# A gated delta rule inside a projection stage: side work pinned between numbered matmuls, decays loaded through GpSimd's queue, and a shorter triangular substitution

## The chip, the cores and the metric

The kernel runs on one core of one Trainium2 chip. The metric is the device time of one execution in microseconds (us); lower is better. In the profile TensorE is PE (its weight loads are PEld), VectorE is DVE, ScalarE is ACT, GpSimd is POOL and SyncE, which issues nearly all DMAs, is SP.

## The reference, cut to what matters

Two decoder layers over 1024 tokens of width 1024. Each layer normalises the residual, projects it once into many pieces, runs a sparse attention branch and a gated delta rule branch, mixes both by gates and projects back. The change concerns the delta rule branch:

```python
qkv_b = jax.nn.silu(causal_depthwise_conv(qkv_b, conv_w[layer]))
q_b = l2_normalize(q_b...); k_b = l2_normalize(k_b...)
beta = jax.nn.sigmoid(beta_l)
g = -jnp.exp(a_log[layer]) * jax.nn.softplus(a_l + dt_bias[layer])
# per head, in chunks:  S_t = a_t (I - b_t k_t k_t^T) S_{t-1} + b_t k_t v_t^T,  o_t = S_t^T q_t,  a_t = exp(g_t)
decay = jnp.exp(jnp.where(incl, gc[..., :, None] - gc[..., None, :], -jnp.inf))
lower = jnp.where(strict, (kb @ k^T) * decay, 0.0);  tmat = I + lower
u, w = triangular_solve(tmat, v * beta), triangular_solve(tmat, kb * exp(gc))
v_new = u - w @ state
o = (q * exp(gc)) @ state + ((q @ k^T) * decay) @ v_new
state = state * g_tot + k_dec^T @ v_new
y_b = rms_norm(o_b, gdn_norm_gain) * silu(z_b)
```

There are 8 heads of width 128. The kernel works in 8 chunks of 128 tokens.

## The kernel before, in words

Each layer has three stages. `token_phase` makes the token-major projections and the top-k selection. `feature_phase` makes, feature-major, the conv inputs of q, k, v and the gates, and runs the delta rule beside them. `attention` does the sparse attention and half of the output projection.

`feature_phase` is the stage that the change touches. It consists of 2208 projection matmuls of 128x128 by 128x512 (`proj_feat`, L361; 24 of them fill one PSUM bank), fed by weights that SP loads (`w_raw`, L303), ACT rounds (`w_hi`, L139) and DVE subtracts (`w_lo`, L140). A head takes 144 of them for its three convolutions (k, q, v in this order) and 96 for its two gates; the gates of a head are projected one head later, in `gdn_finish`. Everything else of a head is side work:

- `decay_rows` loads the head's decay rows, spread to all partitions (512 KB, `H<-rows`, issued by SP at L665), masks them on POOL (L666) and takes the exponent on ACT in eight pieces (L669). The tile `H` has three buffers, so the load for head h+1 waits until head h-2 has finished with its own.
- `gdn_front` convolves (ACT copies L687 and L688, DVE L694 three times, ACT L696, DVE L697), transposes k, q and v (L708), takes their norms (ACT L723), scales `kdec` and `vb` (DVE L713) and forms the products k k^T and q k^T (L758, L760, L761).
- `inverse_blocks` inverts the 32x32 diagonal blocks: it sends them through DRAM into a layout with one row set per partition, does 31 substitution steps of two DVE instructions each on all eight row groups (L847, L849), and sends the result back through DRAM (L851, and 16 small loads at L855).
- `inverse_pairs` joins the blocks by small matmuls (L871 to L893).
- `gdn_chunks` is the recurrence: per chunk `pk` (L780), `r` on DVE, `pu` (L784), `u` on DVE (L786), `pn` (L789), the new state on DVE (L794), and the output from two products in two halves of a bank, which DVE scales and adds (L797 to L803).
- `gdn_finish` scales the output (L821), transposes it (L825), multiplies by the gate and stores it to `yb`.

The order in each engine's queue is not written by hand. A planner orders instructions by priority (the order of the program, shifted by `high_priority(offset)`) and by its own estimate of when their inputs are ready; each engine then works through its queue in order and waits at an instruction whose inputs are late. PE's queue before therefore has the side work wherever the planner expected it to be ready.

Of the kernel before, what the change touches and what calls it, by code (L numbers as in the profile page):

```python
# [25 lines left out]
F32 = mybir.dt.float32  # L26
# [4 lines left out]
AF = mybir.ActivationFunctionType  # L31
# [5 lines left out]
P = 128  # L37
# [31 lines left out]
AHEAD, BEHIND = 1000, -10  # L69
# [17 lines left out]
class Trunk:  # L87
    def __init__(self, ctx, tc, args):
# [10 lines left out]
        self.beside = None  # L99
        ctx.enter_context(self.banks(acc=(1, 2), tr=(1, 2)))  # L100
# [49 lines left out]
    def constants(self, first):  # L150
# [25 lines left out]
        for q in range(4):  # L176
            nc.gpsimd.affine_select(self.xinit[32 * q:32 * q + 32], self.xinit[32 * q:32 * q + 32],
                                    pattern=[[1, 8], [-1, 32]], compare_op=OP.not_equal, fill=1.0, base=8 * q,
                                    channel_multiplier=0)
# [113 lines left out]


# [59 lines left out]
    def proj_feat(self, ws, half, act, evac, tag="acc"):  # L354
# [3 lines left out]
        for k in range(KT):  # L358
            cs = slice((k % 4) * P, (k % 4 + 1) * P)
            for i, (a, b) in enumerate(((0, 0), (0, 1), (1, 0))):  # L360
                self.nc.tensor.matmul(acc, ws[k // 4][a][:, cs], act[b][:, k, hs], start=k == 0 and i == 0,  # L361
                                      stop=k == KT - 1 and i == 2)
        evac(hs, acc)
        self.tick()
# [48 lines left out]
    def decays(self, l, p, raw):  # L413
# [41 lines left out]
        row = p.tile([64, P], F32, name="row")  # L455
        nc.vector.tensor_copy(row, pr[:64, :P])
        self.rows = self.dram.tile([T, 8, P], F32, name="rows")
        nc.sync.dma_start(out=self.rows.rearrange("t h c -> (t h) c"), in_=row)
# [180 lines left out]
    def feature_phase(self, l, ht):  # L639
        nc, tc = self.nc, self.tc  # L640
        self.yb = self.dram.tile([HEADS, P, S], F32, name="yb")
        with tc.tile_pool(name="feat", bufs=1) as p, self.banks(ch=(1, 2), oc=(1, 1), more=(1, 1)):
            XF = p.tile([P, T, 64], F32, name="xf")
            nc.gpsimd.memset(XF, 0.0)
            heads = {}
            E = self.decay_rows(p, 0)
            for h in range(HEADS + 1):
                if h < HEADS:
                    H, E = E, self.decay_rows(p, h + 1) if h + 1 < HEADS else None
                    heads[h] = self.gdn_front(l, p, ht, h, H)  # L650
# [4 lines left out]
                if h:  # L655
                    self.gdn_finish(l, p, ht, heads.pop(h - 1))
                if h < HEADS:
                    self.gdn_chunks(p, heads[h], XF)

    def decay_rows(self, p, h):  # L660
# [4 lines left out]
        nc.sync.dma_start(out=E, in_=ap(self.rows, h * P, [[0, P], [8 * P, T], [1, P]]))  # L665
# [6 lines left out]
    def gdn_front(self, l, p, ht, h, H):  # L672
        nc = self.nc
        w = self.w_in[l]
        feat = self.feat[l]
        kf = p.tile([P, S], F32, name="kf", bufs=3)
        qf = p.tile([P, S], F32, name="qf", bufs=3)
        vv = p.tile([P, S], F32, name="vv", bufs=1)
        for base, dst in ((1024, kf), (0, qf), (2048, vv)):
            ct = (base + h * P) // P  # L680
            cw = lambda j: feat[:, 24 * j + ct:24 * j + ct + 1]
            xp = p.tile([P, S + 4], F32, name="xp", bufs=2)
            nc.gpsimd.memset(xp[:, 0:4], 0.0)

            def evac(hs, acc):
                o = hs.start
                nc.scalar.copy(xp[:, 4 + o:516 + o], acc)  # L687
                nc.scalar.activation(dst[:, hs], acc, AF.Copy, scale=cw(3))  # L688

            ws = self.feat_weights(w, C_QKVB + base + h * P)  # L690
            for half in range(2):
                self.proj_feat(ws, half, ht, evac)
            for j in range(3):
                nc.vector.scalar_tensor_tensor(dst, xp[:, 1 + j:1 + j + S], cw(j), dst, op0=OP.mult, op1=OP.add)  # L694
            th = xp[:, 4:4 + S]
            nc.scalar.activation(th, dst, AF.Tanh, scale=0.5)  # L696
            nc.vector.scalar_tensor_tensor(dst, th, 1.0, dst, op0=OP.add, op1=OP.mult)  # L697

        sm = self.small
        beta, egc, egs = (a[:, :, h] for a in (self.beta, self.egc, self.egs))  # L700
        kdec = p.tile([P, T, P], F32, name="kdec", bufs=2)
        vb = p.tile([P, T, P], F32, name="vb", bufs=2)

        def turn(src, half):
            pt = self.tr()
            for i in range(4):
                c = 4 * half + i
                nc.tensor.transpose(pt[:, i * P:(i + 1) * P], src[:, c * P:(c + 1) * P], self.ident)  # L708
            return pt

        def scaled(dst, pt, col, half):
            cs = slice(4 * half, 4 * half + 4)
            nc.vector.tensor_mul(dst[:, cs], pt.rearrange("p (c d) -> p c d", c=4),  # L713
                                 col[:, cs, None].to_broadcast([P, 4, P]))

        ssq = sm.tile([P, 16], F32, name="g_ssq")
        for i, src in enumerate((kf, qf)):
            for half in range(2):
                pt = turn(src, half)
                for c in range(4):  # L720
                    junk = p.tile([P, P], F32, name="g_junk", bufs=1)
                    col = 8 * i + 4 * half + c
                    nc.scalar.activation(junk, pt[:, c * P:(c + 1) * P], AF.Square, accum_out=ssq[:, col:col + 1])  # L723
                if i == 0:
                    scaled(kdec, pt, egs, half)
        v16 = sm.tile([P, 16], F32, name="g_v16")
# [419 lines left out]
```

## Time and profile before

| | |
|---|---|
| median of 3 runs | 2730.17 us (2725.91 to 2731.36) |
| the profiled execution's own time | 2725.06 us, span 2723.3 us |
| PE busy in the span | 2570.7 us, 94% |
| DVE busy | 1972.8 us, 72% |
| ACT busy | 1316.8 us, 48% |
| POOL busy | 111.9 us, 4% |
| `feature_phase`, first and second layer | about 370 to 1101 us and 1718 to 2455 us |

Busy time is the time in which an engine executed instructions; a matmul's end is modelled, and consecutive matmuls overlap, so a busy PE is read from the distance of the starts. "PEclk" in the views is the granted TensorE clock as a share of 2.4 GHz. A wait is idle time of an engine ahead of an instruction, put down to what ended it.

### The profile page before, as it was taken

How to read it: one execution, taken by the hardware profiler on the slowest of the kernel's cores; microseconds unless marked ns; L12 is line 12 of the kernel's file. 1: busy time of each engine (PE TensorE's matmuls, PEld its weight loads, DVE VectorE, ACT ScalarE, POOL GpSimd, SP SyncE). 2: the span in 40 equal slices, each digit the busy share in tenths (PEclk: the TensorE clock that was granted, in tenths of full speed). 3: DMA queues.
4: the chain of work that ended last, by engine and by line, in shares of the span. 5: the costliest groups of instructions: out<-in, count | busy, mean ns of one | idle time of the engine just before them, and what ended most of it. 6: DMA issues, size and time to landing. Idle time of an engine off the chain costs nothing.

```text
span 2723.3 us, 42939 instructions
## 1 busy us (share of the span) xinstructions
PE 2570.7 (94%) x14854; PEld 2140.5 (79%) x14854; DVE 1972.8 (72%) x5450; ACT 1316.8 (48%) x3169; POOL 111.9 (4%) x398
## 2 busy tenths in 40 slices
PE   7999989999999999999999999898999999999998
PEld 7677778777777888898786777686887778888986
DVE  6677967767787775697366888677676777757965
ACT  5579643343333332697245894433333343227962
POOL 0122000000000000000001210000000000000000
PEclk9999999999999999999999999998899999999999
DMA  3113332222222221531420232321212221226324
GB/s 121 48 66 90 85 87 56 49 51 57 61 51 53 50 73 51 174 105 35 157 65 30 78 101 71 77 63 47 53 42 65 51 57 46 69 63 180 92 68 143
DMA packets 283262, 202.95 MB, mean 75 GB/s; under 512 B 55906, under 2 KB 241188, under 8 KB 283044
## 3 DMA queue, kind: packets, MB, share of 16 engines
q1 hardware_dynamic: 283044, 200.20, 26.2%
q8 instruction: 117, 1.92, 0.3%
q14 instruction: 101, 0.83, 0.1%
HBM read 153.80 MB, written 46.33 MB: 73 GB/s over the span
## 4 chain that ended last, share of the span: by engine, by line
PE 68%; DVE 13%; ACT 7%; DMA 6%; issue 5%; POOL 1%; SPq 0%; DVEq 0%; POOLq 0%; ACTq 0%
PE acc L361 20%; PE acc L338 11%; PE more L361 9%; PE acc L1038 4%; PE wide L1006 4%; PE tr L758 2%; PE tr L1029 2%; ACT t_junk L562 2%; PE out L338 2%; ACT g_junk L723 2%; DMA w_raw<-in_w_in_dram 2%; DVE t_junk L544 2%; DVE w_lo L140 2%; DMA H<-rows 2%; PE tr L708 1%
## 5 line engine op out<-in xcount | busy, mean ns | idle before, releaser
L361 PE MATMUL acc<-hi_t,w_hi 128*128 128x512 f32 x1240 | 502.2, 405 | 8.3 <-DVE gate L629 7.3
L361 PE MATMUL acc<-hi_t,w_lo 128*128 128x512 f32 x1240 | 501.9, 405 | 0.0
L361 PE MATMUL acc<-lo_t,w_hi 128*128 128x512 f32 x1240 | 499.6, 403 | 0.0
L139 ACT CAST w_hi<-w_raw 128x512 fp32r<-128x512 f32 (+1 forms) x336 | 201.1, 602 | 371.0 <-PE acc L361 196.8
L140 DVE TENSOR_TENSOR w_lo<-w_raw,w_hi 128x512 fp32r<-128x512 f32 (+1 forms) x336 | 223.3, 668 | 149.2 <-ACT w_hi L139 136.0
L338 PE MATMUL acc<-w_hi,hi_t 128*128 128x512 f32 (+1 forms) x768 | 285.7, 373 | 12.6 <-ACT w_hi L139 7.3
L338 PE MATMUL acc<-w_lo,hi_t 128*128 128x512 f32 (+1 forms) x768 | 284.5, 371 | 2.1 <-DVE w_lo L140 1.9
L338 PE MATMUL acc<-w_hi,lo_t 128*128 128x512 f32 (+1 forms) x768 | 283.6, 369 | 0.0
L361 PEld LDWEIGHTS acc<-hi_t,w_hi 128*128 128x128 f32 x1240 | 236.7, 191 | 49.8 <-DVE gate L629 8.6
L361 PEld LDWEIGHTS acc<-hi_t,w_lo 128*128 128x128 f32 x1240 | 236.2, 190 | 41.1
L361 PEld LDWEIGHTS acc<-lo_t,w_hi 128*128 128x128 f32 x1240 | 236.3, 191 | 40.9
L562 ACT ACTIVATE t_junk<-scores,t_bits 128x640 f16<-128x640 f32 x248 | 198.8, 802 | 30.8 <-DVE t_bits L554 26.0
L361 PE MATMUL more<-hi_t,w_hi 128*128 128x512 f32 x488 | 198.8, 407 | 4.5 <-ACT kf L688 4.5
L361 PE MATMUL more<-hi_t,w_lo 128*128 128x512 f32 x488 | 199.2, 408 | 0.0
L361 PE MATMUL more<-lo_t,w_hi 128*128 128x512 f32 x488 | 198.3, 406 | 0.0
L338 PEld LDWEIGHTS acc<-w_hi,hi_t 128*128 128x128 f32 x768 | 146.2, 191 | 40.6 <-ACT w_hi L139 10.5
L338 PEld LDWEIGHTS acc<-w_lo,hi_t 128*128 128x128 f32 x768 | 146.7, 191 | 27.4 <-DVE w_lo L140 5.1
L338 PEld LDWEIGHTS acc<-w_hi,lo_t 128*128 128x128 f32 x768 | 146.6, 191 | 22.0 <-issue 1.0
L544 DVE TENSOR_SCALAR_CACHE_REDUCE t_junk<-scores,t_bits 128x1024 f16<-128x1024 f32 (+4 forms) x136 | 153.4, 1128 | 4.3
L849 DVE TENSOR_TENSOR xc<-xc,xtmp 128x248 f32<-128x248 f32 (+30 forms) x496 | 141.8, 286 | 3.1
L847 DVE TENSOR_TENSOR xtmp<-wide,xc 128x248 f32<-128x248 f32 (+30 forms) x496 | 141.6, 285 | 2.7
L806 ACT ACTIVATE o_junk<-vb 128x128 f32<-128x128 f32 x128 | 39.6, 310 | 162.3 <-DVE vb L803 126.3
(344 smaller groups left out, 5478.4 us busy)
## 6 DMA issues: line engine op xcount, KB each, us to landing
w_raw<-in_w_in_dram SPq DMA_DIRECT2D x272, 256.0 KB
qs<-stage SPq DMA_DIRECT2D x32, 256.0 KB
ya_gate<-gate SPq DMA_DIRECT2D x32, 256.0 KB
H<-rows SPq DMA_DIRECT2D x16, 512.0 KB
wide<-hscr SPq DMA_DIRECT2D x64, 128.0 KB
yb<-gate SPq DMA_DIRECT2D x32, 256.0 KB
w_raw<-in_w_out_dram SPq DMA_DIRECT2D x32, 256.0 KB
qraw<-qs SPq DMA_DIRECT2D x32, 256.0 KB
```

What stands on the lines that cost most here:

```text
L139: self.nc.scalar.copy(hi, src)
L140: self.nc.vector.tensor_sub(lo, src, hi.bitcast(F32))
L338: nc.tensor.matmul(acc[t][:, :n], a[:, k, ts], ws[k][b][:, :n], start=k == 0 and i == 0, stop=k == KT - 1 and i == 2)
L361: self.nc.tensor.matmul(acc, ws[k // 4][a][:, cs], act[b][:, k, hs], start=k == 0 and i == 0, stop=k == KT - 1 and i == 2)
L544: nc.vector.tensor_scalar(junk[:, :sc[i].shape[1]], sc[i], thr, 0.0, op0=op, op1=OP.add, accum_out=cnt[:, i:i + 1])
L562: nc.scalar.activation(junk[:, :n], sc[i], AF.Sign, bias=f(bits, i), scale=-1.0, accum_out=cnt[:, i:i + 1])
L723: nc.scalar.activation(junk, pt[:, c * P:(c + 1) * P], AF.Square, accum_out=ssq[:, col:col + 1])
L758: nc.tensor.matmul(pg[:, o0:o0 + P], kf[:, cs], a[:, cs], start=True, stop=True)
L847: nc.vector.tensor_mul(tmp[:, :, j + 1:], ln[:, None, j, j + 1:].to_broadcast(shape), X[:, :, j:j + 1].to_broadcast(shape))
L849: nc.vector.tensor_add(X[:, :, j + 1:], X[:, :, j + 1:], tmp[:, :, j + 1:])
L1006: nc.tensor.matmul(ps[:, :w], qt[a][:, i], kt[b][:, g, o:o + w], start=j == 0, stop=j == 2)
L1038: nc.tensor.matmul(po, a, b[:, cs], start=j == 0 and i == 0, stop=j == t and i == 2)
```

## The change

PE's projection matmuls of the stage are counted (`self.count`), and each piece of a head's side work is traced when the count reaches a position given by a table, relative to the head's first matmul. `issue_after(mm)` keeps the PE instructions of the piece behind that matmul; instructions of the other engines are not held back by it. `high_priority(offset=PLANNED)` puts the piece ahead of other ready work. Beside this:

- `H<-rows` is issued by POOL instead of SP. A second load of the same size and form, `qe` = exp(gc) spread to all partitions, is added; q is multiplied by it once (1024 wide, DVE), so that the two products of the output add up in one PSUM bank. ACT copies the output out and squares it, in place of two DVE instructions per chunk (L802, L803).
- `u` is copied by ACT instead of DVE; `vb` is scaled by ACT in eight pieces instead of by DVE in two; the sums of squares are one 512-wide ACT instruction and a DVE reduction instead of four ACT instructions that accumulate.
- The substitution computes in step j only the first j // 4 + 1 of eight row groups, with rows dealt to partitions in another order. The way back through DRAM takes four stores and four loads instead of one store and 16 loads.
- The matmuls of the two independent block pairs alternate and go to one bank.
- The `xp` buffers are made once, so that POOL no longer clears four columns before every convolution.

```diff
+AT_DECAYS, AT_KEYS, AT_ROW, AT_QUERIES, AT_PRODUCTS, AT_VALUES, AT_PAIRS, AT_CHUNKS, AT_OUTPUTS = (
+    70, (100, 106), 130, (142, 147), (151, 155, 159, 163), (204, 210), 325, 362, 526)
+STEP_PAIRS, STEP_CHUNKS = 6, 7
...
+    def planned(self, mm=None):
+        while True:
+            due = [x for x in self.plan if mm is None or x[0] <= self.count]
+            if not due:
+                return
+            first = min(due, key=lambda x: x[:2])
+            self.plan.remove(first)
+            with ExitStack() as ctx:
+                if mm is not None:
+                    ctx.enter_context(self.tc.issue_after(mm))
+                ctx.enter_context(self.tc.high_priority(offset=PLANNED))
+                first[2]()
...
+        at(AT_DECAYS, lambda: hd.update(qe=self.decay_queries(p, hd)))
+        for half in range(2):
+            at(AT_KEYS[half], lambda half=half: self.gdn_keys(p, hd, half))
+            at(AT_QUERIES[half], lambda half=half: self.gdn_queries(hd, half))
+            at(AT_VALUES[half], lambda half=half: self.gdn_values(p, hd, half))
+        at(AT_ROW, lambda: self.gdn_row(p, hd))
+        for i, pos in enumerate(AT_PRODUCTS):
+            at(pos, lambda i=i: self.gdn_products(p, hd, 2 * i))
+        at(AT_PRODUCTS[-1], lambda: self.gdn_inverse(p, hd))
+        pairs = self.inverse_pairs(p, hd, XF)
+        at(AT_PAIRS, *[lambda: next(pairs, None)] * 6, gap=STEP_PAIRS)
+        chunks = self.gdn_chunks(p, hd)
+        at(AT_CHUNKS, *[lambda: next(chunks, None)] * (3 * T - 1), gap=STEP_CHUNKS)
...
-        nc.sync.dma_start(out=E, in_=ap(self.rows, h * P, [[0, P], [8 * P, T], [1, P]]))
+        nc.gpsimd.dma_start(out=E, in_=ap(self.rows, h * P, [[0, P], [8 * P, T], [1, P]]))
...
+    def gdn_inverse(self, p, hd):
+        self.nc.vector.tensor_mul(hd["qf"], hd["qf"], hd["qe"])
+        with self.tc.high_priority(offset=AHEAD - PLANNED):
+            self.inverse_blocks(p, hd["H"], hd["ccomp"])
+
+    def decay_queries(self, p, hd):
+        qe = p.tile([P, 32, 32], F32, name="wide", bufs=1).rearrange("p a b -> p (a b)")
+        self.nc.gpsimd.dma_start(out=qe.rearrange("p (t c) -> p t c", c=P),
+                                 in_=ap(self.rows, (T * 8 + hd["h"]) * P, [[0, P], [8 * P, T], [1, P]]))
+        return qe
...
-            nc.vector.tensor_copy(u, pu)
+            nc.scalar.copy(u, pu)
+            yield
...
-                nc.tensor.matmul(po[:, P:2 * P], qf[:, cs], st, start=True, stop=True)
-            nc.tensor.matmul(po[:, :P], A[:, c], u, start=True, stop=True)
...
+                nc.tensor.matmul(po, qf[:, cs], st, start=True, stop=False)
+            nc.tensor.matmul(po, A[:, c], u, start=st is None, stop=True)
+            nc.scalar.copy(vb[:, c], po)
...
+        pos = max(hd["at"] + AT_OUTPUTS, self.count + 2)
+        for half in range(2):
+            self.at(pos + STEP_PAIRS * half, lambda half=half: outputs(half))
...
         for j in range(31):
+            n = j // 4 + 1
             tmp = p.tile([P, 8, 32], F32, name="xtmp", bufs=1)
-            shape = [P, 8, 31 - j]
-            nc.vector.tensor_mul(tmp[:, :, j + 1:], ln[:, None, j, j + 1:].to_broadcast(shape),
-                                 X[:, :, j:j + 1].to_broadcast(shape))
-            nc.vector.tensor_add(X[:, :, j + 1:], X[:, :, j + 1:], tmp[:, :, j + 1:])
+            shape = [P, n, 31 - j]
+            nc.vector.tensor_mul(tmp[:, :n, j + 1:], ln[:, None, j, j + 1:].to_broadcast(shape),
+                                 X[:, :n, j:j + 1].to_broadcast(shape))
+            nc.vector.tensor_add(X[:, :n, j + 1:], X[:, :n, j + 1:], tmp[:, :n, j + 1:])
...
+        pairs = [(slice(32 * b, 32 * b + 32), slice(32 * b + 32, 32 * b + 64)) for b in (0, 2)]
+        py = self.bank("ch")
+        for c in range(T):
+            for k, m in pairs:
                 nc.tensor.matmul(py[m, 32 * c:32 * c + 32], H[k, c, m], XF[k, c, 0:32], start=True, stop=True)
```

## Rows read from the trace of the kernel before

**Rows 1.** Stage windows: length, busy us (count) by engine, clock, DMA share, GB/s.

```profile
370.00:1101.00 731.00, 688.51 (x4181) 566.71 (x4179) 523.10 (x1468) 258.92 (x742) 11.58 (x33) 0.97 0.23 58
...
1718.00:2455.00 737.00, 691.04 (x4165) 571.41 (x4163) 521.07 (x1466) 259.03 (x742) 11.51 (x33) 0.96 0.23 57
```

**Rows 2.** PE's waits, first layer's stage: total us, times, longest.

```profile
PE tr L825 <- DVE vb L821: 22.0, 5, 6.0
PE tr L708 <- DVE kdec L713: 7.3, 1, 7.3
```

**Rows 3.** PE's waits, second layer's stage: total us, times, longest.

```profile
PE tr L825 <- DVE vb L821: 25.9, 5, 6.4
PE tr L708 <- DVE kdec L713: 8.2, 3, 7.2
PE ch L871 <- DVE xf L864: 4.5, 1, 4.5
```

**Rows 4.** Timeline of PE over one stall: start, us, instruction, [idle before <- releaser].

```profile
707.15 0.39 PE L361 MATMUL more<-lo_t,w_hi 128*128 128x512 f32 x1
712.68 1.97 PE L825 MATMUL tr<-ident,vb 128*128 128x128 f32 x8 [5.15 <-DVE vb L821]
```

**Rows 5.** Timeline of DVE over the same stall.

```profile
710.68 0.69 DVE L140 TENSOR_TENSOR w_lo<-w_raw,w_hi 128x512 fp32r<-128x512 f32 x1 [5.18 <-ACT w_hi L139]
...
711.41 1.22 DVE L821 TENSOR_TENSOR vb<-vb,rs_y 128x1024 f32<-128x1024 f32 x1
```

**Rows 6.** Timeline of ACT over the same stall.

```profile
707.22 2.45 ACT L669 ACTIVATE H<-H,ngm 128x128 f32<-128x128 f32 x8 [6.84 <-POOL xp L683]
...
710.04 1.12 ACT L139 CAST w_hi<-w_raw 128x512 fp32r<-128x512 f32 x2
```

**Rows 7.** Timeline of POOL ahead of the same stall.

```profile
706.09 1.09 POOL L666 TENSOR_SCALAR_AFFINE_SELECT H<-H 128x1024 f32<-128x1024 f32 x1 [18.80 <-DMA w_raw<-in_w_in_dram]
```

**Rows 8.** Timeline of SP ahead of the same stall.

```profile
697.07 0.37 SPq L665 DMA_DIRECT2D H<-rows  x1
```

**Rows 9.** Windows after two stalls, columns as in rows 1.

```profile
712.00:718.00 6.00, 5.32 (x23) 4.65 (x24) 4.23 (x15) 1.48 (x9) 0.00 (x0) 0.59 0.52 145
...
1895.00:1925.00 30.00, 24.49 (x189) 21.38 (x188) 14.81 (x45) 9.25 (x41) 0.00 (x0) 0.55 0.10 30
```

**Rows 10.** Timeline of PE: one chunk matmul between projections.

```profile
664.51 0.38 PE L784 MATMUL ch<-vb,H 128*128 128x128 f32 x2
664.65 0.48 PE L361 MATMUL more<-hi_t,w_hi 128*128 128x512 f32 x1
664.96 0.39 PE L361 MATMUL more<-lo_t,w_hi 128*128 128x512 f32 x1
665.19 0.40 PE L361 MATMUL more<-hi_t,w_lo 128*128 128x512 f32 x1
```

**Rows 11.** Timeline of PE: block pairs, one pair alone and two alternating.

```profile
492.16 0.59 PE L871 MATMUL ch<-xf,H 32*32 32x32 f32 x13
492.57 0.21 PE L877 MATMUL ch<-H,y 32*32 32x32 f32 x1
...
492.69 0.48 PE L877 MATMUL ch<-H,y 32*32 32x32 f32 x10
```

**Rows 12.** Groups by line, whole span: shapes and count | busy us, mean ns | idle before.

```profile
L849 DVE TENSOR_TENSOR xc<-xc,xtmp 128x248 f32<-128x248 f32 (+30 forms) x496 | 141.8, 286 | 3.1
L847 DVE TENSOR_TENSOR xtmp<-wide,xc 128x248 f32<-128x248 f32 (+30 forms) x496 | 141.6, 285 | 2.7
...
L694 DVE SCALAR_TENSOR_TENSOR kf<-xp,feat,kf 128x1024 f32<-128x1024 f32 x48 | 61.3, 1277 | 7.4 <-ACT kf L688 7.2
...
L803 DVE SCALAR_TENSOR_TENSOR vb<-oc,egc,vb 128x128 f32<-128x128 f32 x112 | 38.7, 346 | 1.0
...
L697 DVE SCALAR_TENSOR_TENSOR kf<-xp,kf 128x1024 f32<-128x1024 f32 x16 | 19.5, 1220 | 27.9 <-ACT xp L696 27.8
...
L696 ACT ACTIVATE xp<-kf 128x1024 f32<-128x1024 f32 x16 | 17.0, 1060 | 17.3 <-DVE kf L694 17.3
```

More of the change, by code (lines that the diff above doesn't have):

```diff
@@ L99, in __init__ @@
         self.beside = None
+        self.plan, self.count = [], 0
         ctx.enter_context(self.banks(acc=(1, 2), tr=(1, 2)))
@@ L360, in proj_feat @@
             for i, (a, b) in enumerate(((0, 0), (0, 1), (1, 0))):
-                self.nc.tensor.matmul(acc, ws[k // 4][a][:, cs], act[b][:, k, hs], start=k == 0 and i == 0,
-                                      stop=k == KT - 1 and i == 2)
+                mm = self.nc.tensor.matmul(acc, ws[k // 4][a][:, cs], act[b][:, k, hs], start=k == 0 and i == 0,
+                                           stop=k == KT - 1 and i == 2)
+                self.count += 1
+                if not (k == KT - 1 and i == 2):
+                    self.planned(mm.ins)
         evac(hs, acc)
+        self.planned(mm.ins)
         self.tick()
@@ L654, in feature_phase, with plan_head @@
                         self.gate_a(l, ht, f)
[L655 to L658, printed above, removed]
+                if before and h < HEADS:
+                    self.gdn_finish(l, p, ht, before)
+            self.planned()
+    def plan_head(self, p, hd, XF):
+        at = lambda pos, *steps, gap=0: [self.at(hd["at"] + pos + i * gap, f) for i, f in enumerate(steps)]
+        at(AT_DECAYS, lambda: hd.update(qe=self.decay_queries(p, hd)))
[11 more added lines that the diff above has]
+        at(AT_CHUNKS, *[lambda: next(chunks, None)] * (3 * T - 1), gap=STEP_CHUNKS)
     def decay_rows(self, p, h):
@@ L670, in decay_rows, with conv @@
         return E
[L672 removed]
+    def conv(self, l, p, ht, hd, name, base, bufs):
         nc = self.nc
[L674 removed]
         feat = self.feat[l]
[L676 to L726, printed above, removed]
[L727 to L737 removed]
@@ new lines, in conv, with turned @@
+        for j in range(3):
+            nc.vector.scalar_tensor_tensor(dst, xp[:, 1 + j:1 + j + S], cw(j), dst, op0=OP.mult, op1=OP.add)
+        th = xp[:, 4:4 + S]
+        nc.scalar.activation(th, dst, AF.Tanh, scale=0.5)
+        nc.vector.scalar_tensor_tensor(dst, th, 1.0, dst, op0=OP.add, op1=OP.mult)
+    def turned(self, src, half):
+        pt = self.tr()
+        for i in range(4):
+            c = 4 * half + i
+            self.nc.tensor.transpose(pt[:, i * P:(i + 1) * P], src[:, c * P:(c + 1) * P], self.ident)
+        return pt
```

200 lines of the change are left out of this document (124 added, 76 removed).

## The prediction, as recorded before the run

> **What bounds the kernel now.** I read the stage windows first. In the stage that the change touches PE is busy for 688.5 of 731 us in the first layer and 691.0 of 737 us in the second, DVE for about 71% and ACT for 35% [rows 1]. So TensorE sets the time, and side work on the other engines matters only where TensorE waits for it. What PE lacks is 42.5 + 46.0 = 88.5 us of idle time.
>
> Next, the waits of PE in these two stretches. In each layer five waits for `vb` (L821) ahead of the output transposes hold 22.0 and 25.9 us; one wait for `kdec` at the start of the stage holds about 7 us; the second layer has one of 4.5 us ahead of the block pairs [rows 2, 3].
>
> The timelines over one of these five waits show what is late. PE starts its last projection at 707.15 and its next instruction, a transpose, at 712.68 [rows 4]. It waits for L821 on DVE, but DVE stood still too: for 5.18 us behind `w_lo`, which waited for `w_hi` on ACT [rows 5]. ACT in turn had reached the eight exponents of the next head's `H` and stood there for 6.84 us; only after them came `w_hi`, at 710.04 [rows 6]. The exponents waited for POOL's mask, which starts at 706.09 [rows 7], and that for the 512 KB load that SP issued at 697.07 [rows 8]: 9.0 us from issue to use. So one late load stops ACT, ACT stops DVE, and DVE stops PE, because each works through its queue in order. The load could not go earlier, as its buffer belongs to head h-2 until that head's last `pu`.
>
> A stall costs more than its idle time. In the 6 us after this one the granted clock is 0.59, so most of it at the lower level, 1.2 GHz; the 5.32 busy us lose 0.41 x 5.32 = 2.2 us. In the second layer a longer stretch of 30 us has a clock of 0.55: 0.45 x 24.49 = 11.0 us [rows 9]. With 2.2 us for each of six stalls in the first layer and five in the second (the sixth L821 or `kdec` stall and the pairs' wait there fall in the long stretch), the clock costs 13 + 11 + 11 = 35 us. What a stage without waits could give back is 88.5 + 35 = about 124 us.
>
> **The change part by part.** *TensorE's own work* stays what it is: 2208 projections per layer, the same transposes, products and chunk matmuls. A chunk matmul put between two projections costs 0.14 us itself and makes the next start 0.31 instead of 0.23 us later, so 0.22 us [rows 10]; before and after, a chunk has three places of insertion. One small matmul per layer is added, below 0.3 us.
>
> *Block pairs.* Alone, 13 instructions of one pair take 0.41 us, 0.0315 us each; where two alternate, six take 0.12 us, 0.020 us each [rows 11]. The two steps that now alternate have 64 such instructions per head: 64 x 0.0115 = 0.74 us, over 16 heads 12 us. The bounds are 0, since the alternating rows write two banks and the change one, and 12; I take 12, as the alternating rows are the nearest. The Trainium skill (TensorEngine Tiling (Array Packing), Gotcha 1: PSUM Pressure) speaks against it: different row tiles cannot access one PSUM bank at a time. By that rule the term would be 0 and the sum 12 us higher; no row here shows two row tiles in one bank.
>
> *DVE and ACT.* The substitution multiplies and adds 1560 instead of 3968 elements per partition and pass. It takes 62 x 0.286 = 17.7 us per head now [rows 12], and saves between nothing and 61% of that. The second output instruction (0.346 us, seven per head) goes [rows 12]; the multiplication of q by `qe` is new, at the 1.22 us of a 1024-wide instruction [rows 5]. All of this lies beside TensorE, on engines at 71% and 35%, and I cost it at nothing: what hides it is the run of projections. If that cover went, DVE's saving could be no more than part of the waits counted above. `u` moves from DVE to ACT, so the recurrence now stands in ACT's queue: behind an ACT that waits for a load, TensorE would wait too, for up to the 5.15 us of rows 4; if ACT is free, nothing.
>
> *The load of `H`.* It leaves SP, where weight loads were queued behind it, for POOL's queue, where the mask and the new `qe` load stand behind it. POOL no longer clears `xp`, so it no longer waits for convolutions. The buffer's release stays: `pu` of the last chunk of head h-2 is planned at 509, which is 29 in head h. How long the load takes from POOL no row shows; below, I bound it by 9.0 us (the row of the same transfer from SP) and by twice that, and take 9.0. ACT's exponents still wait in order. What is late next is the convolution of k, whose evacuation may stand behind them, and with it the key transposes at 100. By the rows: position 29 is reached after 29 x 0.23 + 7 chunk matmuls x 0.22 = 8.2 us. Then the load, the mask 1.09, the exponents 2.45, two ACT passes 1.12 [rows 6, 7], three DVE passes of 1.28, ACT 1.06 and DVE 1.22 [rows 12]: k is ready 8.2 + 9.0 + 10.8 = 28.0 us into the head. Position 100 is reached after 23.0 + 9 x 0.22 + 0.8 for eight transposes (half of 712.68 to 714.30, which ran at the low clock [rows 4]) + two pair steps of 1.0 (32 instructions at 0.0315) = 27.8 us. So the plan all but covers the load (0.2 us short): between positions 29 and 100 TensorE's side work needs nothing of ACT that the load holds up, and the output transposes come at 46 and 52, with their DVE work queued ahead of the late weights. The `qe` load has until position 163, far more than another 9 us.
>
> *What remains.* The `kdec` wait at the start of a layer stays in full, since the first loads and exponents are the same: (7.3 + 2.2) x 2 = 19 us. Head 2 starts at count 384, but head 0's `pu` frees its buffer only at 509; that load falls on the recurrence of head 1, whose `u` is now on ACT: one stall of 5.15 + 2.2 per layer, 15 us. Of the small waits (42.5 - 22.0 - 7.3 = 13 us in the first layer) I keep a quarter: 6 us. Together 40 us.
>
> *The sum.* 124 - 40 = 84 us of stalls, plus 12 us of pairs: 96 us. From the profiled execution's own 2725.1 us that leaves 2629 us; the median of the runs shown is 5 us above that execution, so I predict 2634 us.
>
> **The rivals.** *The wait moves.* ACT still stands still for about 6 us per load, in order, and some position of the plan meets it (keys, pairs, or a `u`). For it: nothing in the change moves the load ahead of its buffer's release, and the sum above leaves no margin. Against it: the positions leave a gap there. With ten waits of 47.9 / 10 = 4.8 us kept, and 2.2 us of clock each, 70 us come back, of which 15 are in the sum already: 2634 + 55 = about 2690 us.
>
> *Nothing changes.* Positions only bound PE's instructions from below; if the planner's estimates still run ahead of the chip by the same time everywhere, the whole lag of a head turns up at another instruction, and the pairs give little: 2718 to 2730 us. Against it: the lag has one cause in all ten stalls, and TensorE has no dependent work placed next to it any more.
>
> *Slower, by one mechanism: the load from POOL's queue lands late.* A stall at the keys lasts the load's time less 8.8 us. The gain of 96 us over ten loads is used up at 9.6 us each, 7.4 of them idle and 2.2 of clock, so from a load of 16 us on the kernel gets slower; at twice the row, 18 us, it is (9.2 + 2.2) x 10 = 114 us above the forecast, 2748 us. For it: the same data from another queue, with 1024 pieces of 512 bytes, and a second such load per head beside it. Against it: the DMA engines are at 23% [rows 1]. The Trainium skill (DMA: Bandwidth & Descriptors, SWDGE vs HWDGE vs iDMA) says that GpSimd's DMAs are set up by software, more slowly than SP's, and that VectorE can keep it from writing descriptors; no run here shows it. The same page's fit (Anatomy of one DMA, 2.0 us plus bytes / 436e3) would give 3.2 us for 512 KB, but the trace has 9.0 from SP, so I do not use it.
>
> **How the numbers follow.** Forecast 0.58, the moved wait 0.20, no change 0.07, slower by the late load 0.15. The lower end is a stage without any wait, with the pairs' 12 us: 2730 - 124 - 12 = 2594 us. The upper end takes in the moved wait and half the way from there to a load at twice the row, 2720 us; what lies beyond holds about 0.2. The forecast's own range is 2605 to 2665 us. Faster by over 0.2% (about what a measurement of this kernel can tell from no change): 0.79; within it 0.07; slower 0.14.
>
> **What would show it.** Right: no idle time of PE ahead of the output transposes; PE busy above 97% of both stages; the clock at 1.00 nearly throughout; ACT still idle ahead of the exponents, with PE running on. The pairs' alternating instructions about 0.020 us apart. Wrong: PE idle ahead of key transposes, pairs or chunk matmuls with ACT or a DMA as the releaser; a gap well over 9 us between a head's `pu` of the last chunk and the mask two heads on; or the block pairs ready later than position 325, so that the recurrence slides into the next head's work.

## The result: slower by 0.85%, and the profile after

The changed kernel takes 2752.0 us (2746.0 to 2758.0) where the kernel before takes 2728.9 us: a ratio of 1.0085, with a 95% interval of 1.0059 to 1.0111. I had predicted 2634 us. The profiled execution is the slowest of its four, 2758.0 us with a span of 2756.3, so its 33 us over the span of before are 23 us in the medians.

The stage windows of the kernel before, here from the stage's first evacuation to its last projection (columns as in [rows 1]):

```profile
374.50:1096.00 721.50, 679.08 (x4136) 559.34 (x4136) 517.35 (x1458) 257.77 (x740) 11.58 (x33) 0.97 0.23 57
1721.10:2450.20 729.10, 685.30 (x4135) 567.14 (x4136) 516.67 (x1458) 257.88 (x740) 11.51 (x33) 0.96 0.23 56
```

The same of the changed kernel, then windows in it: after its first late pair step, and during head 3's way through DRAM:

```profile
374.40:1130.40 756.00, 705.36 (x4147) 573.06 (x4146) 474.27 (x1278) 273.35 (x710) 23.59 (x27) 0.94 0.31 65
1757.70:2485.60 727.90, 691.54 (x4143) 562.97 (x4144) 474.57 (x1278) 273.25 (x710) 23.44 (x27) 0.96 0.30 68
...
483.00:489.00 6.00, 6.00 (x42) 4.02 (x42) 1.57 (x4) 0.00 (x0) 0.00 (x0) 0.50 0.51 141
489.00:495.00 6.00, 6.00 (x70) 4.42 (x70) 0.27 (x1) 2.27 (x5) 0.00 (x0) 0.50 0.00 0
495.00:501.00 6.00, 6.00 (x27) 4.65 (x27) 2.22 (x5) 0.58 (x1) 0.00 (x0) 0.50 0.01 3
...
692.00:695.00 3.00, 3.00 (x15) 2.41 (x14) 2.62 (x14) 0.38 (x3) 0.88 (x1) 1.00 0.84 89
695.00:698.00 3.00, 2.51 (x16) 1.89 (x15) 1.39 (x2) 0.00 (x0) 0.00 (x0) 1.00 0.96 100
698.00:701.00 3.00, 3.00 (x15) 2.40 (x14) 0.00 (x0) 0.49 (x2) 1.09 (x1) 1.00 1.06 210
```

PE's idle time in the two stages was 42.4 + 43.8 = 86.2 us and is 50.6 + 36.4 = 87.0 us: nothing came back. PE's busy time in them rose by 32.5 us, nearly all of the 33.3 us by which the two stages together are longer. All of this lengthening is in the first layer: its stage takes 34.5 us more, at a clock of 0.94 in place of 0.97, the second layer's 1.2 us less. So there are two questions: what took the place of the waits, and why TensorE works longer on the same matmuls.

PE's waits over the whole run of the changed kernel:

```profile
PE ch L965 <- DVE xf L956: 40.0, 21, 6.2
...
PE ch L878 <- ACT g_u L874: 9.8, 2, 5.0
PE tr L910 <- DVE vb L906: 8.7, 12, 1.1
PE tr L797 <- DVE g_nc L788: 8.3, 2, 4.2
```

The five waits a layer ahead of the output transposes, 22.0 and 25.9 us [rows 2, 3], are down to 8.7 us in all. In their place stand 40.0 us ahead of the block pairs. The timeline of the changed kernel over the longest of them, in the first layer's head 0 (SP, POOL, DVE, PE):

```profile
467.36 2.78 SPq L944 DMA_DIRECT2D xscr<-xc  x4
...
479.07 0.34 SPq L929 DMA_DIRECT2D wide<-hscr  x1
479.58 1.97 SPq L947 DMA_DIRECT2D H<-xscr  x4
...
467.42 0.91 POOL L840 DMA_DIRECT2D wide<-rows  x1 [70.77 <-DVE xc L940]
...
467.16 0.17 DVE L940 TENSOR_TENSOR xc<-xc,xtmp 128x8 f32<-128x8 f32 x1
...
477.82 1.23 DVE L833 TENSOR_TENSOR qf<-qf,wide 128x1024 f32<-128x1024 f32 x1 [7.22 <-DMA wide<-rows]
...
482.39 1.36 DVE L956 STREAM_TRANSPOSE xf<-H 32x256 f32<-32x256 f32 x3 [1.34 <-DMA H<-xscr]
...
482.97 0.28 PE L965 MATMUL ch<-xf,H 32*32 32x32 f32 x2 [6.18 <-DVE xf L956]
```

The substitution ends at 467.33. Its last instruction releases two things: the store of the solved blocks (467.36, SP) and, because `qe` is loaded into the buffer that the substitution was reading (`wide`), the 512 KB load of `qe` (467.42, POOL). They run together, the small store in the shadow of the big load: the return `H<-xscr`, which waits for the store, is issued 12.2 us after it. Over the first seven heads of the layer this takes 12.2, 8.0, 11.3, 11.5, 5.3, 5.7 and 11.0 us, a mean of 9.3; in head 3, where the load of `H` runs too (issued at 690.35), the DMA engines are at 84% and more meanwhile, as the windows show. In head 0 the next head's `wide<-hscr` also stands ahead of the return on SP and waits for `qe`'s reader, so the 12.2 us of this head are not the store's alone; in heads 1, 3 and 6 SP waits at the return for the store alone. After the 6.18 us wait PE runs at 0.50, the lower level of 1.2 GHz, for the next 18 us: a late pair step costs more than its wait.

Heads 4 and 5, whose return is issued after 5.3 and 5.7 us, are late for another reason. ACT and DVE in head 4:

```profile
787.49 2.45 ACT L728 ACTIVATE H<-H,ngm 128x128 f32<-128x128 f32 x8 [8.05 <-POOL H L725]
...
791.02 1.28 DVE L750 SCALAR_TENSOR_TENSOR kf<-xp,feat,kf 128x1024 f32<-128x1024 f32 x1 [4.77 <-ACT kf L744]
...
795.54 0.42 DVE L956 STREAM_TRANSPOSE xf<-H 32x256 f32<-32x256 f32 x1
```

ACT has stood for 8.05 us at the exponents of the next `H`, whose load POOL issued at 777.40. Its part of the next head's k convolution (L744) comes behind them, DVE stands 4.77 us for that, and on DVE the transposes of the blocks stand behind the three passes of this convolution. This is the standstill of the kernel before, now met by a pair step. These heads have 13.6 of the 40.0 us: 3.4 and 4.6 in the first layer, 2.7 and 2.9 in the second. The load of `qe` runs beside the return there as well, so both causes are at work at once.

The pitch of plain projection matmuls, first before, then after:

```profile
603.79 0.39 PE L361 MATMUL acc<-hi_t,w_hi 128*128 128x512 f32 x1
604.02 0.39 PE L361 MATMUL acc<-lo_t,w_hi 128*128 128x512 f32 x1
604.25 0.39 PE L361 MATMUL acc<-hi_t,w_lo 128*128 128x512 f32 x1
604.47 0.39 PE L361 MATMUL acc<-hi_t,w_hi 128*128 128x512 f32 x1
604.70 0.39 PE L361 MATMUL acc<-lo_t,w_hi 128*128 128x512 f32 x1
```

```profile
785.32 0.40 PE L387 MATMUL acc<-lo_t,w_hi 128*128 128x512 f32 x1
785.55 0.39 PE L387 MATMUL acc<-hi_t,w_lo 128*128 128x512 f32 x1
785.79 0.40 PE L387 MATMUL acc<-hi_t,w_hi 128*128 128x512 f32 x1
786.02 0.39 PE L387 MATMUL acc<-lo_t,w_hi 128*128 128x512 f32 x1
786.25 0.40 PE L387 MATMUL acc<-hi_t,w_lo 128*128 128x512 f32 x1
```

Four steps take 0.91 us before and 0.93 after. Over all unbroken runs of eight or more in 560 to 720 and 1900 to 2060 us it is 0.2277 us (386 steps) before and 0.2334 (302) after, with the clock at 1.00 and nothing in between. 5376 such matmuls make 5.7 ns about 30 us, of which the 4416 in the two stages have 25. The rest of the longer busy time is the clock: by the stage windows PE loses 0.06 x 705 = 42 us to it in the first layer, where it lost 0.03 x 679 = 20. That is an estimate from rounded clocks; 25 + 22, less 12 for the pairs (below), make 35 us where 32.5 are measured.

### The profile page after: what moved, and what is told of

Same layout as the page of the kernel before. It is cut to its first block, busy times and chain, and to the rows that moved or that the text cites. A ratio compares the mean times of both kernels' runs of the same rounds, so it can differ in the third digit from the quotient of the medians.

```text
span 2756.3 us, 42183 instructions
## 1 busy us (share of the span) xinstructions
PE 2610.9 (95%) x14858; PEld 2148.0 (78%) x14858; DVE 1882.4 (68%) x5082; ACT 1344.8 (49%) x3107; POOL 135.8 (5%) x386
## 4 chain that ended last, share of the span: by engine, by line
PE 64%; DVE 16%; DMA 7%; issue 6%; ACT 5%; POOL 1%; SPq 1%; DVEq 0%; POOLq 0%; ACTq 0%
PE acc L387 18%; PE acc L364 11%; PE more L387 8%; PE acc L1137 4%; PE wide L1105 4%; PE tr L1128 2%; ACT t_junk L595 2%; PE out L364 2%; DMA xscr<-xc 2%; PE tr L826 2%; DVE xc L940 2%; DVE xtmp L938 2%; DVE w_lo L148 2%; PE out L387 2%; PE wide L544 1%
## 5 line engine op out<-in xcount | busy, mean ns | idle before, releaser
L387 PE MATMUL acc<-hi_t,w_hi 128*128 128x512 f32 x1240 | 510.8, 412 | 9.6 <-DVE gate L662 5.1
L387 PE MATMUL acc<-lo_t,w_hi 128*128 128x512 f32 x1240 | 514.5, 415 | 0.0
L387 PE MATMUL more<-lo_t,w_hi 128*128 128x512 f32 x488 | 205.0, 420 | 0.0
L364 PEld LDWEIGHTS acc<-w_hi,lo_t 128*128 128x128 f32 x768 | 147.5, 192 | 22.6 <-issue 1.0
L387 PEld LDWEIGHTS more<-hi_t,w_hi 128*128 128x128 f32 x488 | 94.8, 194 | 23.2 <-ACT qf L744 3.2
L940 DVE TENSOR_TENSOR xc<-xc,xtmp 128x60 f32<-128x60 f32 (+24 forms) x496 | 104.4, 210 | 11.7
L938 DVE TENSOR_TENSOR xtmp<-wide,xc 128x60 f32<-128x60 f32 (+24 forms) x496 | 104.1, 210 | 11.0
```

The source lines that it names most:

```text
L364: nc.tensor.matmul(acc[t][:, :n], a[:, k, ts], ws[k][b][:, :n], start=k == 0 and i == 0, stop=k == KT - 1 and i == 2)
L387: mm = self.nc.tensor.matmul(acc, ws[k // 4][a][:, cs], act[b][:, k, hs], start=k == 0 and i == 0, stop=k == KT - 1 and i == 2)
L938: nc.vector.tensor_mul(tmp[:, :n, j + 1:], ln[:, None, j, j + 1:].to_broadcast(shape), X[:, :n, j:j + 1].to_broadcast(shape))
L940: nc.vector.tensor_add(X[:, :n, j + 1:], X[:, :n, j + 1:], tmp[:, :n, j + 1:])
```

## Experiments

Ratios are to the kernel before, timed on the same chip beside each. The changed kernel's is 1.0085.

**Pitch: where the weight buffers stand.** The change renames and shrinks some tiles in the pool of small tiles, so the weight buffers behind it start 192 bytes earlier. An unused column moves them:

```diff
+        pad = self.small.tile([P, 16], F32, name="pad", bufs=1)
+        self.nc.vector.memset(pad, 0.0)
```

That is 64 bytes (e1); e8 and e11 have 128 and 512, e12 has 64 in the first pool, ahead of the activations, and e2 has 192 in the changed kernel.

> The kernel before, with an unused 64-byte column per partition in the pool of small tiles, so that the weight buffers (and all tiles after them) start at SBUF byte 94336 of a partition in place of 94272: at a multiple of 128 as in the changed kernel, where before they stood 64 bytes past one. Theory A (the weights' place in SBUF sets the pace of the projection matmuls): pitch 0.2267 goes to about 0.2333 us, and 5376 projection matmuls x 6.6 ns make about 2729 + 35 = 2764 us. Rival B (the pace comes from something else in the changed program): pitch stays 0.2267, 2726 to 2731 us.

> The kernel before with an unused 128-byte column in the pool of small tiles: the weight buffers at byte 94400, again 64 past a multiple of 128 as in the kernel before, but on other bytes than there. If what counts is the place against a multiple of 128: pitch 0.2267 and 2725 to 2735 us, no change. If any shift against the other tiles costs: pitch 0.230 to 0.2333 and about 2744 us, as with 64 bytes.

> The kernel before with an unused 512-byte column in the pool of small tiles: the weight buffers and all behind them 512 bytes further, the distance from the activations' buffer to the weights again a multiple of 512 (100928 - 24128 = 150 x 512; before 149 x 512). If that distance within 512 bytes sets the pitch: 0.2267 and 2722 to 2732 us. If it is any other property of the place: 0.230 to 0.234 and 2737 to 2745 us, as with 64 and 128 bytes.

> The kernel before with an unused 64-byte column in the first pool, ahead of the activations' buffers: activations and weights move by 64 bytes together. If their distance sets the pitch: 0.2267 and 2722 to 2732 us. If the place of the weights itself does (64 past a multiple of 128): 0.230 to 0.234 and 2737 to 2745 us.

> The changed kernel with an unused 192-byte column in the pool of small tiles, so that the weight buffers stand at the very byte of the kernel before (94272). Theory A: pitch 0.2333 goes back to 0.2267, PE busy falls by about 40 us, about 2752 - 35 = 2717 us. Rival B: pitch stays 0.2333 and 2752 us.

| kernel | distance of weights from activations, modulo 512 bytes | pitch, us | ratio (95%) |
|---|---|---|---|
| before | 0 | 0.2277 | 1 |
| e1, 64 bytes | 64 | 0.2333 | 1.0048 (1.0030 to 1.0067) |
| e8, 128 bytes | 128 | 0.2328 | 1.0056 (1.0037 to 1.0075) |
| e11, 512 bytes | 0 | 0.2278 | 1.0002 (0.9992 to 1.0013) |
| e12, both moved by 64 | 0 | 0.2277 | 1.0003 (0.9993 to 1.0014) |
| changed | 320 | 0.2334 | 1.0085 (1.0059 to 1.0111) |
| e2, changed + 192 bytes | 0 | 0.2279 | 1.0077 (1.0055 to 1.0100) |

The distances come from the layout of the tile pools, not from the traces; the expectations put the pitch before at 0.2267 us, and it is 0.2277. The pitch follows the distance of the two operands' buffers modulo 512 bytes, as far as it was tried: 0.228 us at 0, 0.233 at the other three. A remainder of 256 was not tried, so the period could be 256. What counts is not the weights' own place (e8 keeps it 64 past a multiple of 128 and is slow; e12 loses that and is fast). In the kernel before, a distance other than 0 costs 13 to 15 us, less than half of the 35 expected in e1. In the changed kernel e2 restores the pitch and wins nothing: PE's busy time falls from 2610.9 to 2577.0 us, but its idle time rises from 145.4 to 163.9. So the layout is a cause by itself, but while the blocks come late a faster TensorE only waits for them longer.

**Late pairs: moving them in the plan.** e3 moves the load of `qe` from 70 to 95 of its head, e4 adds the pad, e5 moves pairs, chunks and outputs 25 matmuls later, e6 adds the pad to that.

```diff
-    70, ... 325, 362, 526)
+    95, ... 325, 362, 526)      (e3, e4)
+    70, ... 350, 387, 551)      (e5, e6)
```

> The changed kernel with the load of the spread query decays (512 KB on GpSimd's queue) placed at matmul 95 of its head in place of 70, behind the first pair step of the head before (85), so that it no longer shares the DMA engines with the return of that head's blocks. If the load is what makes the blocks late: the 40.0 us of waits for xf go below 10, with the clock that follows them some 10 us more, 2752 - 40 = 2712 us (2700 to 2722). Rival (the return is late by itself, since DVE ends the substitution late): the waits stay above 30 us and the time within 2746 to 2756.

> The changed kernel with both edits, the 192-byte pad and the load at 95. Both theories right: 2752 - 35 - 40 = 2677 us. Only the load: 2712. Only the place in SBUF: 2717. Neither: 2752.

> The changed kernel with the block pairs, the chunks and the outputs 25 matmuls later in the plan (350, 387, 551 in place of 325, 362, 526), some 5.8 us. Theory C (the pairs are due before the blocks are back, and the 40 us of waits for xf with the slow clock behind them are what the plan lost): waits for xf below 8 us, granted clock up from 0.969 to 0.973 or more, 2752 - 32 - 10 = 2710 us (2700 to 2722). Rival D (the lateness is only handed on: the state's buffers come free 5.8 us later, so the load of H and the products at 151 are late next): waits for H and for chunks take the place, 2745 to 2760 us.

> The same with the 192-byte pad, which puts the weight buffers where the kernel before has them. Theories A and C together: pitch of 0.228 in place of 0.233 (5376 projection matmuls, about 25 us) on top of C's 2710: 2685 us (2675 to 2700). If the faster pitch only makes side work late, as in the padded kernel without the later slots (2751 us): about 2710, the same as without the pad.

e3: 1.0103 (1.0086 to 1.0120), waits for `xf` 42.3 us. e4: 1.0064 (1.0042 to 1.0085), 42.9 us. The position didn't move the load, as POOL's timeline in e3 shows:

```profile
778.72 0.91 POOL L724 DMA_DIRECT2D H<-rows  x1 [74.63 <-ACT g_u L874]
787.98 1.09 POOL L725 TENSOR_SCALAR_AFFINE_SELECT H<-H 128x1024 f32<-128x1024 f32 x1 [8.35 <-DMA xscr<-xc]
789.02 0.91 POOL L840 DMA_DIRECT2D wide<-rows  x1
```

A position holds back PE's instructions alone. The load starts when its buffer is free and POOL's queue lets it, here right behind the mask; so neither theory was tested.

e5: 1.0113 (1.0091 to 1.0134). The waits for `xf` fall to 14.4 us, and 57.3 us appear ahead of the output transposes. DVE's timeline in e5 shows why:

```profile
790.26 0.43 DVE L956 STREAM_TRANSPOSE xf<-H 32x256 f32<-32x256 f32 x1 [1.41 <-DMA H<-xscr]
...
792.30 1.22 DVE L906 TENSOR_TENSOR vb<-vb,rs_y 128x1024 f32<-128x1024 f32 x1
```

The transposes of the late blocks stand ahead of the output's multiplication on DVE, which works in order; PE, which reached the output transposes, waits 7.44 us for it. The lateness is handed on, as rival D said, though at another place. e6: 1.0116 (1.0091 to 1.0141), the same.

**Late pairs: the load of the query decays.** e7 leaves it out; e9 and e10 (with the pad) hold it back behind the first pair step by a copy on DVE, e13 by a sum that also reads the transposes' result:

```diff
-        self.nc.gpsimd.dma_start(out=qe..., in_=ap(self.rows, ...))
+        self.nc.gpsimd.memset(qe, 1.0)                                              (e7)
+        nc.vector.tensor_copy(late, hd["ln"][:, 0, 0:1])                            (e9, e10)
+        nc.vector.tensor_add(late[:96], hd["ln"][:96, 0, 0:1], XF[:96, 0, 0:1])     (e13)
```

> The changed kernel without the second load on GpSimd's queue: the spread query decays (512 KB a head) are left out and the tile is filled with ones by GpSimd (so the queries' decay is left out of the outputs). Theory E (that load, issued behind the mask just as the blocks come back, slows the return from 2 us to 6 or 7): waits for xf fall from 40.0 to below 12 us, about 2752 - 28 - 8 = 2716 us. Rival F (the blocks are late before that, since VectorE ends the substitution late): waits for xf stay above 28 us, 2740 to 2752 us.

> The changed kernel with nothing left out, in which the load of the query decays can't start before the blocks are back: a 128x1 copy of the tile that it fills stands behind the transposes of the first pair step on VectorE, so the load waits for them (its place in the plan goes from 70 to 95, behind that step). Theory E (this load slows the return of the blocks): waits for xf fall from 40.0 to 18 us or less, as without the load; 2752 - 45 = 2707 us (2697 to 2717), faster than the kernel before. Rival G (it is now late for its own reader, the product with the queries at 163, 18 us after): VectorE's queue stands still there and the products or the substitution wait, 2735 to 2755 us.

> The same with the 192-byte pad, which puts the weight buffers at the byte of the kernel before. If the shorter pitch comes through once the blocks are not late: 2707 - 20 = 2687 us (2677 to 2697). If side work sets the pace by now: about 2707.

> The changed kernel, nothing left out, with the load of the query decays really held back: a 96x1 sum on VectorE reads the tile that the load fills and the result of the transposes in the first pair step, so the load can start only behind these. Theory E (the load, and nothing else that was left out with it, slows the return of the blocks): on GpSimd's queue the load stands some 9 us later than in the changed kernel, waits for xf fall from 40 to about 18 us, PE idle from 145 to about 118, the clock from 0.970 to 0.976: 2752 - 45 = 2707 us (2697 to 2720). Rival G (it then lands too late for the product with the queries): that product, and the products queued behind it on VectorE, wait; 2735 us or more.

e7: 0.9911 (0.9884 to 0.9939), some 47 us below the changed kernel. SP's timeline in e7, head 0, and PE's waits of the whole run:

```profile
462.72 2.58 SPq L943 DMA_DIRECT2D xscr<-xc  x4
465.46 0.94 SPq L928 DMA_DIRECT2D wide<-hscr  x2
466.74 1.79 SPq L946 DMA_DIRECT2D H<-xscr  x4
```

```profile
PE ch L964 <- DVE xf L955: 17.6, 12, 2.6
```

From store to return it now takes 4.0, 4.0, 3.9, 6.0, 5.5, 5.3 and 5.2 us, a mean of 4.8 in place of 9.3. The stages idle for 59.3 us (87.0 after) and are busy for 1374.7 (1396.9), with the clock at 0.97 in both. SP's own waits show the store directly; the changed kernel, then e7, whole runs (us, times, longest):

```profile
SPq L947 <- DMA xscr<-xc: 31.4, 19, 5.6
SPq L946 <- DMA xscr<-xc: 10.4, 20, 1.8
```

The 17.6 us that e7 still waits for `xf` are no collision with `qe`, and more than the 12 expected. All of them are in heads 3, 4 and 5 of the two layers, and the chain is the one of head 4 above. ACT and DVE in e7, head 4:

```profile
756.33 2.45 ACT L728 ACTIVATE H<-H,ngm 128x128 f32<-128x128 f32 x8 [8.18 <-POOL H L725]
...
759.87 1.29 DVE L750 SCALAR_TENSOR_TENSOR kf<-xp,feat,kf 128x1024 f32<-128x1024 f32 x1 [4.92 <-ACT kf L744]
...
764.40 1.36 DVE L955 STREAM_TRANSPOSE xf<-H 32x256 f32<-32x256 f32 x3
```

The return was issued at 756.83, and DVE doesn't stand still ahead of the transposes: they are late by their place in its queue. The same chain has the waits left in e13 (heads 4 and 5) and in e15 (heads 3 to 5), below. The traces show it; no run takes it away, so what it costs with its clock isn't measured.

e9 and e10: 1.0088 (1.0061 to 1.0114) and 1.0081 (1.0063 to 1.0099). The copy needed only the substitution's input, so it ran at its start (846.64, in e9), and the load went out as early as ever; these two tell nothing of the load. e13: 0.9991 (0.9976 to 1.0005), 26 us below the changed kernel with nothing left out. Waits for `xf` are 13.3 us. POOL's timeline in e13:

```profile
766.13 1.09 POOL L725 TENSOR_SCALAR_AFFINE_SELECT H<-H 128x1024 f32<-128x1024 f32 x1 [8.30 <-DMA H<-rows]
777.04 0.91 POOL L840 DMA_DIRECT2D wide<-rows  x1 [9.82 <-DMA w_raw<-in_w_in_dram]
```

The load waits 9.8 us behind the mask, and the return, issued at 768.35, is over by then. So the collision itself costs, as theory E says; why e13 stays 21 us above the 2707 us expected isn't settled. SP waits there for 28.4 us at `wide<-hscr` until this load has landed, against 10.4 in the changed kernel, so the load is now late for others.

**The part undone, and the rest of the plan.** e14 undoes the query decays: the state part of the output is scaled on DVE again, with nothing left out. e15 adds the 192-byte pad. On e15 as a base, e16 moves pairs, chunks and outputs 12 later, e17 puts the load of `H` back on SP, and e18 makes the substitution long again.

```diff
-        self.nc.vector.tensor_mul(hd["qf"], hd["qf"], hd["qe"])
...
-                nc.tensor.matmul(po, qf[:, cs], st, start=True, stop=False)
+                nc.tensor.matmul(po[:, P:2 * P], qf[:, cs], st, start=True, stop=True)
...
+                nc.vector.scalar_tensor_tensor(vb[:, c], po[:, P:2 * P], self.egc[:, c, h:h + 1], vb[:, c], ...)
...
-        nc.gpsimd.dma_start(out=E, in_=ap(self.rows, h * P, ...))                   (e17)
+        nc.sync.dma_start(out=E, in_=ap(self.rows, h * P, ...))
...
-            n = j // 4 + 1                                                          (e18)
+            n = 8
```

> The changed kernel with one part undone and nothing left out: no spread query decays, no load of them and no product with the queries; the chunk's state part is scaled as before on VectorE (one 128x128 operation a chunk, 0.35 us, less the 1.23 us a head), and its two matmuls go to two halves of the bank again. Theory E: as without the load, about 2702 us, plus at most some us for VectorE's 112 x 0.35 - 16 x 1.23 = 20 us of work beside the matmuls: 2705 us (2697 to 2715). Rival F (what helped was the shorter queue of VectorE, not the free DMA engines): 2740 us or more, since VectorE has more to do here.

> The same with the 192-byte pad, so that the distance from the activations' buffer to the weights is a multiple of 512 bytes again. Theories A and E together: some 20 us below the one without the pad, 2685 us (2675 to 2697). If side work sets the pace: about 2705.

> The fastest version so far (the part on query decays undone, 192-byte pad: 2702 us) with pairs, chunks and outputs 12 matmuls later (337, 374, 538), 2.7 us. Its waits for xf are 22.8 us, the longest 3.6. If they come from the slot alone: below 8 us, 2702 - 15 - 10 (clock) = 2677 us (2670 to 2690). If lateness is only handed on (as when all moved 25 later with the load still there): other waits take the place, 2698 to 2710 us.

> That version of 2702 us with the load of H back on SP's queue, as in the kernel before. If GpSimd's queue is what took the load's wait for a free buffer off the weights' path: the loads of weights and the blocks' return behind it on SP wait for the last chunks of a head, the stalls before products and projections come back, 2715 to 2740 us. If the queue makes no difference: 2702 us.

> That version of 2702 us with the substitution over all eight rows at each step, as long as in the kernel before (some 4.6 us a head more on VectorE: 208.5 against 283.4 us over 16 heads). If VectorE's work is hidden here, as the prediction took it to be: 2702 us. If the substitution stands on the path to the pairs: each of the 12 waits for xf grows by up to 4.6 us, and heads that had none get one, waits for xf 60 to 90 us, 2750 us or more.

e14: 0.9932 (0.9909 to 0.9955), although DVE has more to do (1893.0 against 1882.4 us): rival F falls. e15: 0.9888 (0.9864 to 0.9913), 2702.4 us, well below both kernels; the pitch is 0.2278 again and is now worth 11 us. Stage windows and PE's largest wait by total in e15:

```profile
373.80:1086.60 712.80, 678.49 (x4145) 558.12 (x4145) 478.83 (x1326) 281.15 (x710) 16.64 (x19) 0.97 0.27 63
1709.70:2427.80 718.10, 682.81 (x4144) 561.01 (x4144) 479.32 (x1326) 281.34 (x710) 16.49 (x19) 0.96 0.27 63
```

```profile
PE ch L968 <- DVE xf L959: 22.8, 12, 3.6
```

e16: 0.9901 (0.9883 to 0.9920). The waits for `xf` are gone from the list's head, and 44.3 us stand ahead of the output transposes, behind the blocks' transposes on DVE as in e5: handed on again. In heads 3 to 5 the load of `H` goes out about 1 us ahead of the store there, and the return follows the store by 9.4 to 11.3 us: another 512 KB load at this moment does what `qe`'s did. e17: 0.9878 (0.9855 to 0.9902), no difference from e15; which queue loads `H` is worth nothing here, against my expectation. e18: 1.0011 (1.0002 to 1.0020), 31 us above e15: neither hidden nor the 48 us or more expected on the path to the pairs, and not where expected. The waits for `xf` are 15.0 us, not 60 to 90, and the transposes of k, q and v (L761) wait 18.8 us for the convolution of k and 21.5 us for other work of DVE. The substitution in e18, by lines:

```profile
L943 DVE TENSOR_TENSOR xc<-xc,xtmp 128x248 f32<-128x248 f32 (+30 forms) x496 | 143.6, 290 | 8.2
L941 DVE TENSOR_TENSOR xtmp<-wide,xc 128x248 f32<-128x248 f32 (+30 forms) x496 | 143.6, 289 | 8.5
```

In e15 the two take 103.8 and 104.2 us. So the shorter substitution, 79 us of DVE's time, is worth 31 us.

## Why the prediction was wrong, by its own steps

- **The stalls for `vb`.** Right. 47.9 us became 8.7. But PE does not always run on while ACT waits for the load; the third point has where.
- **The load of `H`.** It was put at 9.0 us by the row of SP; from POOL the median is 9.1. The rival of a late load from POOL named the right sign and nearly the right time (2748 us) by luck: its mechanism, ten loads of 16 us or more that stall the keys, doesn't occur, and e17 finds the queue without effect. In e15 one wait a layer (7.1 and 8.0 us) does stand ahead of the key transposes, at the layer's start, where ACT waits with the exponents for the first loads.
- **"Between positions 29 and 100 TensorE's side work needs nothing of ACT that the load holds up."** This step failed. The pair steps of the head before begin at 325 - 240 = 85, and the working counts them as 1.0 us each but not as readers. They need DVE's transposes, which DVE has behind the k convolution, and that needs ACT. By the prediction's own terms the third pass of that convolution ends 8.2 + 9.0 + 1.09 + 2.45 + 1.12 + 3 x 1.28 = 25.7 us into the head, and position 85 is reached after 85 x 0.23 + 9 x 0.22 + 0.8 = 22.3 us: 3.4 us late. In heads 4 and 5 the pairs waited 2.7 to 4.6 us a head, 13.6 in all, with `qe`'s load there too; where that load is gone, this chain alone holds PE for 17.6 (e7) to 22.8 us (e15).
- **"The `qe` load has until position 163, far more than another 9 us."** This step failed too, and cost most of what a run measured. I asked when the load's reader needs it, not when the load runs and beside what. Its buffer is the substitution's, so it starts with the store of the blocks, the most urgent transfer of the stage. In the working of the sum the blocks' return has no due time; "the block pairs ready later than position 325" is only in the last paragraph. It cost about 26 us (e13, where the load only goes out later) to 47 us (e7, where it is left out).
- **"TensorE's own work stays what it is."** Failed too: same matmuls, another pitch, from 192 bytes in the layout. That costs 13 to 15 us in the kernel before (e1, e8) and 11 us once the pairs are not late (e15 against e14).
- **DVE and ACT "at nothing".** Wrong for the substitution: with each step placed by a count and no slack behind it, DVE's order decides, and e18 gives 31 us. The clause that named it ("if that cover went") bounded it by the waits counted, and 31 us is inside that bound, but the sum had it at 0.
- **Block pairs, 12 us.** Right. L871 and L877 took 22.6 + 22.7 us; L965 and L972 take

```profile
L965 PE MATMUL ch<-xf,H 32*32 32x32 f32 x512 | 16.8, 209 | 40.0 <-DVE xf L956 40.0
L972 PE MATMUL ch<-H,y 32*32 32x32 f32 x512 | 16.4, 216 | 0.0
...
797.50 0.69 PE L965 MATMUL ch<-xf,H 32*32 32x32 f32 x30 [1.16 <-DVE xf L956]
```

so 12.1 us less. Thirty of them take 0.69 us from the first start to the last end, at most 0.023 us each, against 0.0315 from start to start alone [rows 11], though both row tiles write one bank. The rule of the Trainium skill (TensorEngine Tiling (Array Packing), Gotcha 1: PSUM Pressure), that different row tiles cannot access one bank at a time, did not show here.
- **What remains, 40 us.** Head 2's late `H` was right: 4.8 and 5.0 us at the chunks against 5.15. The wait at a layer's start stayed too, at other instructions: 9.5 us in the first layer in place of 7.3. The small waits were too low: even e7, without the collision, idles for 59 us in the stages, e15 for 69.6.
- **The clock, 35 us.** Not given back: 0.97 and 0.96 before, 0.94 and 0.96 after, 0.97 and 0.96 in e15. The longest late pair step is followed by 18 us at the lower level, as the old stalls were by such stretches [rows 9].

- **The rivals.** The wait did move: the idle time of the stages is what it was. That rival named the pairs as one of three places and ACT's standstill behind the load of `H` as the cause. This is right for 13.6 of the 40.0 us ahead of the pairs, and for all 17.6 that are left of them in e7. The other 26.4 us are nearly all in heads where the load of `qe` runs beside the store or the return, which no rival named as a cause, and the 2690 us left out the pitch.

Of the predicted 96 us, e15 brings 30 in the medians. In the profiled executions its stages have 16.6 us less idle time than before. Why PE's busy time there falls by only 3 us, when the pairs alone give 12, is not settled; in e15 the projections together take 2186.9 us against 2176.1. The idle time that e15 has left is known in its larger parts: 22.8 us ahead of the pairs, 15.1 at the layers' starts, 11.8 at the chunks (L878, for ACT); no run took these away.

## What to carry to other kernels

For each new transfer ask what releases it: one that takes over a scratch buffer starts the moment the scratch's last reader ends, together with the transfer that carries the result away. Before a wait is called covered, list every step that falls into its window, those of other heads too, with each engine that the step needs and what stands ahead of it there. A position in a plan holds back only the engine whose instructions it counts; to move a load, give it another buffer or a dependence on what must come first. After any edit that adds or drops a tile, compare the pitch of the matmuls that were not touched, before looking for a reason in the edit.

## What the runs showed of the hardware

The pitch of 128x512 matmuls is 0.228 us where the buffers of the moving and the stationary operand lie a multiple of 512 bytes apart, and 0.233 us at a remainder of 64, 128 or 320: 2.5% for a few bytes of padding. After a wait of 6.2 us PE was busy for 18 us at the lower clock. Beside a 512 KB load it took 8 to 11.5 us from a store of 4 x 32 KB to the issue of its reader (heads 1, 3 and 6 of the changed kernel, with SP waiting for the store alone), and 4 to 6 us in e7, where that load is left out.
